# A decoder trunk on one core: loads in another order, first sums of the second group earlier, low halves between norm steps

## The chip, the cores and the metric

The kernel runs on one core of a Trainium2 chip. A core has TensorE (PE) for matrix products, VectorE (DVE), ScalarE (ACT), GpSimd (POOL) and SyncE (SP), which here only issues transfers. Each engine works through its own instructions in order; semaphores order them against each other. The metric is device time in microseconds (us), the median of several executions.

## The reference

The function is a trunk of two layers over 256 tokens of width 1024. Each layer is an FFN, a mixer, and a second FFN, each between two RMS norms and added to x:

```python
hdn = swiglu(rms_norm(x, norm_pre[l, 0]), ffn1_w_gate[l], ffn1_w_up[l], ffn1_w_down[l])
x = x + 0.5 * rms_norm(hdn, norm_post[l, 0])
h = rms_norm(x, norm_pre[l, 1])
...
x = x + rms_norm(mix, norm_post[l, 1])
hdn = swiglu(rms_norm(x, norm_pre[l, 2]), ffn2_w_gate[l], ffn2_w_up[l], ffn2_w_down[l])
x = x + 0.5 * rms_norm(hdn, norm_post[l, 2])

def swiglu(h, w_gate, w_up, w_down):
    return (jax.nn.silu(h @ w_gate) * (h @ w_up)) @ w_down
```

D_FF is 2816. The mixer of layer 0 ("ab") has one input projection to q, k, v (8 heads of 64, causal softmax over the 256 tokens, rotary on a quarter of a head) and to a recurrent group: causal convolution of width 4, a gated linear recurrence, times gelu of a gate branch; one output projection. The mixer of layer 1 ("c") is B * conv3(C * x~) between two projections. All is float32.

## The kernel before, in words

**Precision.** Every float32 operand of a projection is split into a high half (a rounding to fp32r on ScalarE) and a low half (source minus high half on VectorE, L98, `low`). A product is three matmuls: high by high, high by low, low by high (`mm3`, L261 to L263; `proj_a`, L272 to L277, with tokens on the output's partitions, 512 columns wide; `proj_b`, L289 to L291, with features there, 256 wide).

**Weights.** All weights are read once, in chunks of 1 MB, in one list `chunks`, whose order is the order of SP's queue. A chunk lands in one of two rings of raw buffers, 'a' and 'b' (tiles `ra` and `rb`), each of two tiles. `low` frees a raw tile as soon as its low half is made and then calls `pump`, which issues the next chunks (L89) as long as the next one's ring has a free tile. Since the queue keeps the order of the list, a chunk whose own ring has room still goes after the one ahead of it. Five pairs of high and low halves exist (HL). `prep` makes the high half of the next chunk (ACT, L126), and puts its low half on a list `late`; `flush` issues what is on that list. `done(i, n)` gives a pair back and lets `prep` make up to n further ones.

**FFN.** The 2816 hidden features are 11 column blocks of 256. Blocks 0 and 1 are computed in `first(t)`, once for each half t of the tokens; blocks 2 to 10 in a loop over j in `rest`: gate by `proj_b`, tanh on ACT (L449), t1 (L451) on VectorE, up by `proj_b`, h (L460), and then a part of the down product. For the first eight blocks of w_down rows the down product is a scheme of seven products of half-size blocks instead of eight, for which sums of row blocks and of h blocks are needed. `mix(j)` makes the sums of h (L363, L364, L366) and their halves (M and e). `add(i)` makes the sums of the rows: L143 and L144 on VectorE, then two accumulating transfers on POOL's queue (L145, L146), one after the other. `begin(i)` makes their high halves on ACT (L151, L152). `five(b)`, in the loop at j = b + 2, does five of the products, 15 matmuls of 512 columns. The other two (`two`) and the plain down products of blocks 8 to 10 (`plain`) follow as the second group, in the last blocks and in `tail`. In each turn of the loop, VectorE's order ends with `five(j-2)`'s successor `add(d1[j])` for the rows two blocks on.

**Mixers.** In "ab" the scores are made for the first half of tokens, then for the second (`score`), with softmax on ACT (L616), VectorE (L618) and POOL (L619); the gelu of the gate branch (L580 to L585) reads its product from a PSUM bank; v is a `proj_a`, and heads are then transposed and multiplied (`turn_p`). `bank()` hands out PSUM banks from a list `ring` in turn. Outside of these, `stile`, `etile` and `ptile` hand out SBUF tiles in turn. In "c", `first` ends with zz (L771), which the transposition for the convolution reads.

**Norms and boundaries.** `post_add` (L229, L231) adds a stage's normed output to x, `pre_norm` (L239) norms x for the next stage, `trans_x` (L246, L253, L258) transposes it into high and low halves `xh`, `xl`, and `close` (L408) adds the two groups of products. The gains `gpre` and `gpost` are read by a transfer that gives each of the 128 partitions a copy of the row (`load_gain`, L211).

## Time and profile before

| | |
|---|---|
| median of 3 runs | 1074.96 us (1074.94 to 1082.31) |
| profiled execution | 1072.48 us |
| its span | 1070.7 us |
| mean granted clock of TensorE | 0.961 |
| TensorE busy | 960.1 us (90%) |
| VectorE busy | 737.7 us (69%) |
| ScalarE busy | 503.1 us (47%) |
| GpSimd busy | 103.9 us (10%) |

The span is cut by the stages: FFN of layer 0 to about 257 us, mixer "ab" to 396, FFN to 567, FFN of layer 1 to 767, mixer "c" to 885, FFN to the end; the first 28 us of a stage hold the norms and `first`. A row of the timeline is start, duration, engine, line, operation, tiles by name without numbers, and in brackets the idle time of the engine just before, with what ended it. Matmuls overlap, so their rows give durations longer than their distances. The granted clock falls to half in stretches after TensorE stood.

### The profile page before, as it was taken

How to read it: one execution, taken by the hardware profiler on the slowest of the kernel's cores; microseconds unless marked ns; L12 is line 12 of the kernel's file. 1: busy time of each engine (PE TensorE's matmuls, PEld its weight loads, DVE VectorE, ACT ScalarE, POOL GpSimd, SP SyncE). 2: the span in 40 equal slices, each digit the busy share in tenths (PEclk: the TensorE clock that was granted, in tenths of full speed). 3: DMA queues.
4: the chain of work that ended last, by engine and by line, in shares of the span. 5: the costliest groups of instructions: out<-in, count | busy, mean ns of one | idle time of the engine just before them, and what ended most of it. 6: DMA issues, size and time to landing. Idle time of an engine off the chain costs nothing.

```text
span 1070.7 us, 14796 instructions
## 1 busy us (share of the span) xinstructions
PE 960.1 (90%) x6084; PEld 855.4 (80%) x6084; DVE 737.7 (69%) x833; ACT 503.1 (47%) x594; POOL 103.9 (10%) x129
## 2 busy tenths in 40 slices
PE   6868788799988997999998979999989999799997
PEld 4767677787776887988986978898769988798895
DVE  5456654677767857787768667777767586687675
ACT  5432343355594644454464543455543354444541
POOL 3101000000025001010000001100000010010000
PEclk9997889899998999999999989999999999899999
DMA  9565556488523366778775677786855455778851
GB/s 325 143 187 147 157 161 199 119 299 281 198 98 102 119 216 187 234 203 251 246 256 182 180 224 194 234 257 227 275 175 209 164 177 154 223 216 244 242 198 62
DMA packets 132052, 213.24 MB, mean 199 GB/s; under 512 B 4630, under 2 KB 90646, under 8 KB 131984
## 3 DMA queue, kind: packets, MB, share of 16 engines
q1 hardware_dynamic: 122368, 195.05, 52.8%
q0 software_dynamic: 9616, 17.24, 10.1%
q8 instruction: 48, 0.79, 0.3%
q14 instruction: 20, 0.16, 0.0%
HBM read 194.44 MB, written 1.05 MB: 183 GB/s over the span
## 4 chain that ended last, share of the span: by engine, by line
PE 41%; DMA 23%; DVE 19%; issue 8%; ACT 6%; SPq 1%; POOL 1%; DVEq 0%; POOLq 0%; ACTq 0%
DMA rb<-in_ffn_w_down_dram 17%; DVE lo L98 11%; PE b L289 6%; PE b L291 6%; PE b L290 6%; PE b L262 4%; PE b L263 4%; PE b L261 4%; PE b L277 3%; PE b L272 3%; PE b L273 3%; ACT hi L126 2%; DMA rb<-rb 2%; DMA gpre<-in_norm_pre_dram 2%; DVE P L143 2%
## 5 line engine op out<-in xcount | busy, mean ns | idle before, releaser
L291 PE MATMUL b<-xh,lo 128*128 128x256 f32 x1344 | 376.2, 280 | 5.8 <-DVE lo L98 5.8
L289 PE MATMUL b<-xh,hi 128*128 128x256 f32 x1344 | 377.7, 281 | 4.0 <-ACT hi L126 1.6
L290 PE MATMUL b<-xl,hi 128*128 128x256 f32 x1344 | 375.6, 279 | 0.0
L98 DVE TENSOR_TENSOR lo<-ra,hi 128x2048 fp32r<-128x2048 f32 (+1 forms) x115 | 250.7, 2184 | 52.7 <-ACT hi L126 51.3
L289 PEld LDWEIGHTS b<-xh,hi 128*128 128x128 f32 x1344 | 253.2, 188 | 7.2 <-DVE s L771 2.0
L291 PEld LDWEIGHTS b<-xh,lo 128*128 128x128 f32 x1344 | 253.2, 188 | 6.7 <-DVE lo L98 6.7
L290 PEld LDWEIGHTS b<-xl,hi 128*128 128x128 f32 x1344 | 252.4, 188 | 1.7
L126 ACT CAST hi<-ra 128x2048 fp32r<-128x2048 f32 x107 | 203.6, 1903 | 10.9 <-DMA ra<-in_ffn_w_down_dram 3.4
L262 PE MATMUL b<-lo,M 128*128 128x512 f32 x272 | 115.7, 425 | 56.8 <-DVE lo L98 56.8
L98 DVE TENSOR_TENSOR lo<-rb,hi 128x2048 fp32r<-128x2048 f32 (+1 forms) x74 | 155.8, 2112 | 10.8 <-ACT hi L126 10.8
L365 ACT CAST M<-H 128x640 fp32r<-128x640 f32 x32 | 23.3, 728 | 222.8 <-DVE H L364 222.8
L261 PE MATMUL b<-hi,M 128*128 128x512 f32 x272 | 111.8, 411 | 5.6 <-ACT hi L151 5.6
L262 PEld LDWEIGHTS b<-lo,M 128*128 128x128 f32 x272 | 54.3, 200 | 75.5 <-DVE lo L98 64.0
L263 PE MATMUL b<-hi,M 128*128 128x512 f32 x272 | 112.5, 413 | 0.0
L272 PE MATMUL b<-hi,xh 128*128 128x512 f32 x208 | 86.4, 415 | 8.3 <-DVE e L585 8.3
L143 DVE TENSOR_TENSOR P<-rb 128x512 f32<-128x512 f32 x32 | 22.1, 690 | 104.0 <-DMA rb<-in_ffn_w_down_dram 104.0
L273 PE MATMUL b<-lo,xh 128*128 128x512 f32 x208 | 85.9, 413 | 0.5 <-DVE lo L98 0.5
L151 ACT CAST hi<-rb 128x2048 fp32r<-128x2048 f32 x32 | 61.0, 1905 | 24.4 <-DMA rb<-rb 18.1
L126 ACT CAST hi<-rb 128x2048 fp32r<-128x2048 f32 x35 | 66.7, 1905 | 6.9 <-DMA rb<-in_ffn_w_down_dram 6.1
L261 PEld LDWEIGHTS b<-hi,M 128*128 128x128 f32 x272 | 54.1, 199 | 18.1 <-ACT hi L151 6.2
L145 POOL DMA_DIRECT2D rb<-rb x32 | 27.9, 871 | 403.4 <-DVE s L451 267.2
L263 PEld LDWEIGHTS b<-hi,M 128*128 128x128 f32 x272 | 54.6, 201 | 12.2
(185 smaller groups left out, 1065.4 us busy)
## 6 DMA issues: line engine op xcount, KB each, us to landing
rb<-in_ffn_w_down_dram SPq DMA_DIRECT2D x46, 1024.0 KB, 7.7
ra<-in_ffn_w_gate_dram SPq DMA_DIRECT2D x39, 1024.0 KB, 5.6
ra<-in_ffn_w_up_dram SPq DMA_DIRECT2D x39, 1024.0 KB, 5.7
rb<-rb POOLq DMA_DIRECT2D x64, 256.0 KB, 3.7
ra<-in_ffn_w_down_dram SPq DMA_DIRECT2D x14, 1024.0 KB, 5.0
rb<-in_c_w_in_dram SPq DMA_DIRECT2D x6, 1024.0 KB, 6.3
ra<-in_c_w_in_dram SPq DMA_DIRECT2D x6, 1024.0 KB, 6.7
rb<-in_ab_w_in_dram SPq DMA_DIRECT2D x5, 1024.0 KB, 6.5
```

Source lines behind the costliest of these rows:

```text
L98: eng.tensor_tensor(dst_lo, src, src_hi.bitcast(FT), op=OP.subtract)
L126: act.copy(hi[i], raw[i])
L143: dve.tensor_tensor(t3[i], r[:, 3], r[:, 1], op=OP.add)
L151: act.copy(hi[i], raw[i])
L261: pe.matmul(o, sh, mh, start=start, stop=False)
L262: pe.matmul(o, sh, ml, start=False, stop=False)
L263: pe.matmul(o, sl, mh, start=False, stop=stop)
L272: pe.matmul(o, xh[:, n * 4 + k, ts], hi[i][:, k], start=n * 4 + k == 0, stop=False)
L273: pe.matmul(o, xh[:, n * 4 + k, ts], lo[i][:, k], start=False, stop=False)
L289: pe.matmul(o[:, c], hi[i][:, k, cs], xh[:, k], start=k == 0, stop=False)
L290: pe.matmul(o[:, c], hi[i][:, k, cs], xl[:, k], start=False, stop=False)
L291: pe.matmul(o[:, c], lo[i][:, k, cs], xh[:, k], start=False, stop=k == KT - 1)
```

## The change

It has seven parts.

1. In the list of chunks, the rows of w_down for a block stand between its gate and its up, and those of the second block (d1[1]) stand ahead of the gate of j = 3. They were last of the three.
2. `first(1)` prepares one more gate, without its low half at once, and does `add(d1[1])`; `mix(1)` and a flush move to the front part of the turn j = 2; `add(d1[1])` was in that turn.
3. `flush` can issue a given number of low halves, and such calls stand between the steps of the norms at the boundaries; several `done` calls no longer issue their low halves at once.
4. The gains of the next stage are loaded after `first(1)` (`gpre`, `gpost`), no more at the boundary.
5. At the start, the gain of the first norm is one row, copied to all partitions by two matmuls with a row of ones into PSUM, with eight transpositions of the identity ahead of them; it was a transfer to 128 partitions.
6. The mixers' small parameters are loaded on SP's queue in the turns j = 3 and 4 (`hooks`), not on POOL's at the start; their arithmetic is spread over four turns, up to seven small VectorE steps each.
7. In mixer "ab", `ring` is [7, 4, 6, 5] for v and the heads; the second softmax's scaling is eight VectorE steps and no POOL steps; a low half that POOL made (`flush(pool)`) is made by VectorE later. In mixer "c", zz goes ahead of two low halves.

The diff, cut to what the prediction speaks of:

```diff
-    def flush(eng=dve):
-        while late:
+    def flush(eng=dve, n=99):
+        while late and n:
             low(*late.pop(0), eng)
+            n -= 1
...
         for j in range(2, NB):
-            gu[j] = (cols8(wg, j * 256, "a"), cols8(wu, j * 256, "a"))
-            if j - 2 < NS:
+            if j == 3:
+                d1[1] = rows7(wd, 1)
+            g = cols8(wg, j * 256, "a")
+            if j - 2 < NS and j != 3:
                 d1[j - 2] = rows7(wd, j - 2)
+            gu[j] = (g, cols8(wu, j * 256, "a"))
...
             if t == 1:
                 done(g01[0], n=1)
-                done(g01[1], n=0)
                 turn(0)
+                done(g01[1], n=1, now=False)
+                add(d1[1])
...
                 begin(d1[0])
+                flush()
...
                 mix(0)
                 flush()
-                prep()
...
-                dve.scalar_tensor_tensor(t1, th, 1.0, g, op0=OP.add, op1=OP.mult)
-                flush()
                 if j == 2:
-                    add(d1[1])
-                done(gu[j][0], n=1)
+                    flush()
+                    done(gu[j][0], now=False, n=1)
+                    dve.scalar_tensor_tensor(t1, th, 1.0, g, op0=OP.add, op1=OP.mult)
+                    mix(1)
+                    flush()
+                else:
+                    dve.scalar_tensor_tensor(t1, th, 1.0, g, op0=OP.add, op1=OP.mult)
+                    flush()
+                    done(gu[j][0], n=1)
...
                     flush()
-                    if j == 2:
-                        mix(1)
...
-                done(dn[b])
+                done(dn[b], now=b < NB - 1)
...
-            done(d2[4])
+            done(d2[4], now=False)
+            flush(n=1)
...
+            def scale(n):
+                for _ in range(n):
+                    e, r = scales.pop(0)
+                    dve.tensor_scalar(e, e, r, None, op0=OP.mult)
...
-            def after():
-                done(cg[1], hold=True)
-                flush(pool)
-                lru(0)
-
-            gelu(p, after)
+            gelu(p, lambda: scale(4))
+            scale(4)
+            lru(0)
...
+            ring[:] = [7, 4, 6, 5]
             vs = [etile(512) for _ in range(2)]
...
-                done(gc01[0])
-                done(gc01[1])
+                done(gc01[0], now=False)
+                done(gc01[1], now=False)
...
-    load_gain(gpre, npre[0, 0])
+    act.dma_start(row, npre[0, 0:1])
...
+    gain = [bank("y00"), bank("y01")]
+    for n in range(8):
+        pe.transpose(gain[n // 4][:, 0:128], ident, ident)
+    for h in range(2):
+        pe.matmul(gain[h], ones, row[:, h * 512:h * 512 + 512], start=True, stop=True)
...
+        if n < len(subs) - 1:
+            load_gain(gpre, npre[(n + 1) // 3, (n + 1) % 3])
+        if n:
+            load_gain(gpost, npost[n // 3, n % 3])
         s["rest"]()
...
-            if not last:
-                load_gain(gpre, npre[(n + 1) // 3, (n + 1) % 3])
...
-        done(left)
+        flush(n=1)
+        done(left, now=False)
...
-            load_gain(gpost, npost[(n + 1) // 3, (n + 1) % 3])
             xn = pre_norm(1)
+            flush()
```

What that makes of the queues is seen in three places. SP's queue in the first FFN's blocks, before (`ra` and `rb` are the two raw rings):

```order
L89 DMA ra_453<-in_ffn1_w_gate_dram 128x8x256
L89 DMA ra_539<-in_ffn1_w_up_dram 128x8x256
L89 DMA rb_541<-in_ffn1_w_down_dram 128x2x1024
L89 DMA ra_622<-in_ffn1_w_gate_dram 128x8x256
L89 DMA ra_714<-in_ffn1_w_up_dram 128x8x256
L89 DMA rb_716<-in_ffn1_w_down_dram 128x2x1024
```

And SP's queue of the changed kernel in the same blocks, with the small parameters among the weights:

```order
L89 DMA ra_459<-in_ffn1_w_gate_dram 128x8x256
L89 DMA rb_461<-in_ffn1_w_down_dram 128x2x1024
L89 DMA ra_549<-in_ffn1_w_up_dram 128x8x256
L89 DMA ra_621<-in_ffn1_w_gate_dram 128x8x256
L89 DMA rb_623<-in_ffn1_w_down_dram 128x2x1024
L895 DMA e_688<-in_lru_conv_w_dram 4x512
L895 DMA e_688<-in_lru_conv_b_dram 1x512
L895 DMA e_688<-in_lru_gate_a_b_dram 1x512
L895 DMA e_688<-in_lru_gate_x_b_dram 1x512
L895 DMA e_688<-in_lru_lambda_dram 1x512
L895 DMA e_688<-in_c_conv_w_dram 6x512
L89 DMA ra_712<-in_ffn1_w_up_dram 128x8x256
```

The number behind a tile counts up with the program's instructions, so nearly equal numbers mean two transfers that one step lets go: before, up and rows (539, 541), now gate and rows (459, 461).

VectorE's order in the first turns of the third FFN stage, before (L98 are the low halves, `rb_4831` the rows of the second block):

```order
L98 TENSOR_TENSOR lo_4870<-rb_4647,hi_4869 128x2048
L98 TENSOR_TENSOR P_4872<-P_4791,P_4871 128x512
L98 TENSOR_TENSOR M_4907<-H_4833,M_4907 128x640
L98 TENSOR_TENSOR e_4908<-H_4833,e_4908 128x256
L98 TENSOR_TENSOR lo_4919<-ra_4709,hi_4918 128x2048
L451 SCALAR_TENSOR_TENSOR s_4950<-s_4948,b5_4875 128x512
L143 TENSOR_TENSOR P_4952<-rb_4831 128x512
L144 TENSOR_TENSOR rb_4831<-rb_4831 128x512
L98 TENSOR_TENSOR lo_4958<-ra_4829,hi_4957 128x2048
L460 SCALAR_TENSOR_TENSOR H_5014<-s_4950,b7_4965 128x2x256
```

VectorE's order there in the changed kernel, where `rb_4723` holds the rows of the second block:

```order
L418 SCALAR_TENSOR_TENSOR s_4841<-s_4840,b6_4815 128x512
L98 TENSOR_TENSOR lo_4845<-ra_4708,hi_4844 128x2048
L143 TENSOR_TENSOR P_4862<-rb_4723 128x512
L144 TENSOR_TENSOR rb_4723<-rb_4723 128x512
L428 SCALAR_TENSOR_TENSOR s_4892<-s_4841,b4_4867 128x512
L98 TENSOR_TENSOR lo_4860<-ra_4738,hi_4859 128x2048
L98 TENSOR_TENSOR lo_4895<-rb_4647,hi_4894 128x2048
L98 TENSOR_TENSOR P_4897<-P_4810,P_4896 128x512
```

The sums of the second block's rows (L143, L144) stood in the turn j = 2, behind t1; they now stand in `first(1)`, between t1 and hs of the token half (L418, L428).

SP's queue in the second FFN's blocks, before:

```order
L89 DMA ra_3441<-in_ffn2_w_gate_dram 128x8x256
L89 DMA ra_3513<-in_ffn2_w_up_dram 128x8x256
L89 DMA rb_3515<-in_ffn2_w_down_dram 128x2x1024
L89 DMA ra_3596<-in_ffn2_w_gate_dram 128x8x256
L89 DMA ra_3668<-in_ffn2_w_up_dram 128x8x256
L89 DMA rb_3670<-in_ffn2_w_down_dram 128x2x1024
```

And SP's queue there in the changed kernel:

```order
L89 DMA ra_3460<-in_ffn2_w_gate_dram 128x8x256
L89 DMA rb_3527<-in_ffn2_w_down_dram 128x2x1024
L89 DMA ra_3534<-in_ffn2_w_up_dram 128x8x256
L89 DMA ra_3615<-in_ffn2_w_gate_dram 128x8x256
L89 DMA rb_3682<-in_ffn2_w_down_dram 128x2x1024
L89 DMA ra_3689<-in_ffn2_w_up_dram 128x8x256
```

Here up and rows were let go by one step (3513, 3515); now rows go at a step of their own (3527), a few instructions ahead of up (3534).

More of the change, by code (lines that the diff above doesn't have):

```diff
@@ L231, in post_add, with pre_norm @@
             dve.scalar_tensor_tensor(xres[t][:, cs[h]], yg[h], r, xres[t][:, cs[h]], op0=OP.mult, op1=OP.add)
-    def pre_norm(t, then=None):
+    def pre_norm(t, then=None, gain=None):
+        gain = gain or [gpre[:, 0:512], gpre[:, 512:1024]]
         xn = [stile() for _ in range(2)]
@@ L238, in pre_norm @@
         for h in range(2):
[L239 to L240 removed]
+            dve.scalar_tensor_tensor(xn[h], xres[t][:, h * 512:h * 512 + 512], r, gain[h], op0=OP.mult, op1=OP.mult)
         return xn
@@ L545, in rest @@
         def rest():
-            ring[:] = [4, 5, 6, 7]
             xc = []
@@ L610, in score, with softmax @@
                         soft.append((e, mx, per, nk))
-            def softmax():
+            scales = []
+            def softmax(eng=None):
                 while soft:
@@ L618, in softmax @@
                     dve.reciprocal(mx[:, 2], mx[:, 1])
-                    pool.tensor_tensor(e, e, mx[:, 2, :, None].to_broadcast([128, per, nk]), op=OP.mult)
+                    if eng is None:
+                        scales.extend((e[:, n], mx[:, 2, n:n + 1]) for n in range(per))
+                    else:
+                        eng.tensor_tensor(e, e, mx[:, 2, :, None].to_broadcast([128, per, nk]), op=OP.mult)
+            def scale(n):
+                for _ in range(n):
+                    e, r = scales.pop(0)
+                    dve.tensor_scalar(e, e, r, None, op0=OP.mult)
             gates, decay = [], [stile((128, 2, SEQ)) for _ in range(2)]
@@ L649, in between @@
                 gate(1)
-                softmax()
+                softmax(pool)
                 gate2(1)
@@ L724, in rest @@
                         split(m[2][0], m[2][1], ge[0])
+                        done(cg[1], hold=True)
                         scan(1)
@@ L816, in rest @@
         def rest():
-            ring[:] = [4, 5, 6, 7]
             gate(0)
@@ L835, in trunk @@
     act.activation(mhalf, mhalf, AF.Copy)
+    row = gpre[0:1]
+    ones = st.tile([1, 128], FT, name="ones")
+    pool.memset(ones, 1.0)
     for h in range(2):
         sp.dma_start(xres[0][:, h * 512:h * 512 + 512], x[0, 0:128, h * 512:h * 512 + 512])
-    load_gain(gpre, npre[0, 0])
+    act.dma_start(row, npre[0, 0:1])
     dma()
@@ L843, in trunk @@
     make_identity(nc, ident)
-    xn = pre_norm(0)
+    gain = [bank("y00"), bank("y01")]
[3 more added lines that the diff above has]
+        pe.matmul(gain[h], ones, row[:, h * 512:h * 512 + 512], start=True, stop=True)
+    xn = pre_norm(0, gain=gain)
     need(0)
@@ L849, in trunk @@
     pieced(4)
-    xn = pre_norm(1, lambda: (need(2), pieced(4)))
+    xn = pre_norm(1, lambda: (need(2), pieced(4)), gain)
     need(3)
@@ L893, in params, with step @@
         pool.tensor_tensor(a[:, 3], a[:, 2], a[:, 1], op=OP.pow)
-    def params2():
-        a = spw
-        dve.tensor_scalar(a[:, 4], a[:, 3], 2.0, None, op0=OP.add)
-        dve.reciprocal(a[:, 4], a[:, 4])
-        dve.tensor_tensor(a[:, 4], a[:, 3], a[:, 4], op=OP.mult)
-        dve.tensor_tensor(a[:, 5], a[:, 4], a[:, 4], op=OP.mult)
-        dve.memset(a[:, 6], 1.0 / 17)
-        for n in (15, 13, 11, 9, 7, 5, 3, 1):
-            dve.tensor_tensor(a[:, 6], a[:, 6], a[:, 5], op=OP.mult)
-            dve.tensor_scalar(a[:, 6], a[:, 6], 1.0 / n, None, op0=OP.add)
-        dve.tensor_tensor(a[:, 6], a[:, 6], a[:, 4], op=OP.mult)
-        dve.tensor_scalar(a[:, 7], a[:, 0], 0.0, 2.0, op0=OP.max, op1=OP.mult)
-        dve.scalar_tensor_tensor(sp2, a[:, 6], 4.0, a[:, 7], op0=OP.mult, op1=OP.add)
-        dve.tensor_scalar(sp4, sp2, -2.0, None, op0=OP.mult)
-    hooks += [lambda: None, params, params2]
+    a = spw
+    steps = [lambda: dve.tensor_scalar(a[:, 4], a[:, 3], 2.0, None, op0=OP.add),
+             lambda: dve.reciprocal(a[:, 4], a[:, 4]),
+             lambda: dve.tensor_tensor(a[:, 4], a[:, 3], a[:, 4], op=OP.mult),
+             lambda: dve.tensor_tensor(a[:, 5], a[:, 4], a[:, 4], op=OP.mult),
+             lambda: dve.memset(a[:, 6], 1.0 / 17)]
+    for odd_n in (15, 13, 11, 9, 7, 5, 3, 1):
+        steps += [lambda: dve.tensor_tensor(a[:, 6], a[:, 6], a[:, 5], op=OP.mult),
+                  lambda n=odd_n: dve.tensor_scalar(a[:, 6], a[:, 6], 1.0 / n, None, op0=OP.add)]
+    steps += [lambda: dve.tensor_tensor(a[:, 6], a[:, 6], a[:, 4], op=OP.mult),
+              lambda: dve.tensor_scalar(a[:, 7], a[:, 0], 0.0, 2.0, op0=OP.max, op1=OP.mult),
+              lambda: dve.scalar_tensor_tensor(sp2, a[:, 6], 4.0, a[:, 7], op0=OP.mult, op1=OP.add),
+              lambda: dve.tensor_scalar(sp4, sp2, -2.0, None, op0=OP.mult)]
+    def step():
+        for _ in range(min(7, len(steps))):
+            steps.pop(0)()
+    hooks += [lambda: None, loads1, loads2, params, step, step, step, step]
     then = None
```

34 lines of the change are left out of this document (18 added, 16 removed).

## The prediction

> **What bounds the kernel now.** I began with the page's busy table, then cut the span into stages with the table of stretches, then asked which waits TensorE ends on, and last read single places on the timeline.
>
> ```profile
> PE 960.1 (90%) x6084; PEld 855.4 (80%) x6084; DVE 737.7 (69%) x833; ACT 503.1 (47%) x594; POOL 103.9 (10%) x129
> ```
>
> TensorE is the bound: 960.1 of 1070.7 us busy. What can be won is the 110.6 us in which it stands, and the time in which it runs at half clock. The table of stretches shows where both lie (stretch, its length, busy us of PE, PEld, DVE, ACT, POOL, then granted clock, DMA share, GB/s):
>
> ```profile
> 38.00:200.00 162.00, 120.59 (x784) 110.03 (x784) 91.69 (x128) 56.40 (x55) 13.15 (x15) 0.86 0.55 161
> 200.00:257.00 57.00, 54.72 (x336) 48.03 (x335) 40.66 (x34) 32.08 (x31) 1.50 (x2) 1.00 0.68 245
> 257.00:285.00 28.00, 24.03 (x106) 18.82 (x105) 20.92 (x32) 12.19 (x17) 1.57 (x4) 1.00 0.63 206
> 285.00:339.00 54.00, 45.40 (x312) 40.96 (x312) 42.76 (x55) 38.92 (x81) 19.65 (x11) 0.94 0.44 151
> 396.00:432.00 36.00, 29.52 (x210) 27.57 (x209) 26.42 (x33) 14.37 (x16) 3.45 (x4) 0.91 0.66 195
> 432.00:567.00 135.00, 131.52 (x897) 120.11 (x896) 99.38 (x98) 70.47 (x66) 10.15 (x12) 1.00 0.74 234
> 567.00:595.00 28.00, 25.40 (x107) 19.85 (x106) 20.74 (x24) 9.72 (x18) 3.18 (x4) 0.94 0.61 186
> 595.00:634.00 39.00, 32.61 (x228) 30.28 (x227) 27.75 (x36) 17.70 (x20) 3.44 (x4) 0.91 0.67 195
> 634.00:767.00 133.00, 130.40 (x893) 119.55 (x893) 98.72 (x96) 69.64 (x65) 10.05 (x12) 1.00 0.75 236
> 767.00:797.00 30.00, 25.73 (x108) 19.70 (x106) 19.56 (x21) 12.79 (x19) 1.56 (x6) 0.94 0.59 194
> 885.00:930.00 45.00, 37.98 (x252) 34.38 (x251) 30.42 (x37) 19.81 (x23) 4.29 (x5) 0.92 0.61 174
> 930.00:1063.50 133.50, 130.15 (x887) 119.00 (x885) 94.42 (x93) 61.82 (x58) 9.50 (x11) 1.00 0.67 205
> ```
>
> The first FFN's column blocks (38 to 200) are the outlier: 41 us idle, clock 0.86. The three later FFN stages (396 to 567, 595 to 767, 885 to 1063.5) lose 6 to 7 us at their first blocks and about 3 after. The table of waits of TensorE (line, what it waited for, us in total, times, longest) names the ends:
>
> ```profile
> PE b L262 <- DVE lo L98: 58.6, 21, 7.2
> PE b L246 <- DVE s L239: 14.4, 4, 9.1
> PE b L272 <- DVE e L585: 8.3, 1, 8.3
> PE b L277 <- DVE xl L258: 5.3, 3, 1.8
> ```
>
> More than half of the idle time is L262 inside `five`, waiting for the low half of its rows of w_down. Why VectorE is late with it, the timeline of VectorE, SyncE's queue and TensorE shows in one block of the first stage (the row at 137.59 is from the chain of waits, the next block's rows):
>
> ```profile
> 123.49 0.69 DVE L143 TENSOR_TENSOR P<-rb 128x512 f32<-128x512 f32 x1 [7.95 <-DMA rb<-in_ffn_w_down_dram]
> 125.42 2.28 DVE L98 TENSOR_TENSOR lo<-rb,hi 128x2048 fp32r<-128x2048 f32 x1
> ...
> 115.56 0.37 SPq L89 DMA_DIRECT2D ra<-in_ffn_w_up_dram  x1
> 116.03 0.52 SPq L89 DMA_DIRECT2D rb<-in_ffn_w_down_dram  x1
> ...
> 137.59 7.51 DMA rb<-in_ffn_w_down_dram
> ...
> 127.76 0.79 PE L262 MATMUL b<-lo,M 128*128 128x512 f32 x1 [6.25 <-DVE lo L98]
> ```
>
> VectorE is in order. It stands 7.95 us at L143, which adds up rows for a later block, and behind it stands the low half (125.42) which TensorE needs now. The rows were issued at 116.03 only, behind `up` in the same queue, and `up` waited for a buffer that VectorE frees with its low halves. A loop thus closes over VectorE, SP and a transfer of 7.5 us, and one turn of it takes 137.59 − 116.03 = 21.6 us.
>
> **What the change does, part by part.** First the rate of TensorE without gaps, from a later block:
>
> ```profile
> 479.25 0.28 PE L289 MATMUL b<-xh,hi 128*128 128x256 f32 x1
> 490.56 0.39 PE L261 MATMUL b<-hi,M 128*128 128x512 f32 x1
> ...
> 494.71 0.40 PE L263 MATMUL b<-hi,M 128*128 128x512 f32 x1
> 494.94 0.28 PE L289 MATMUL b<-xh,hi 128*128 128x256 f32 x1
> ```
>
> The 96 products of gate and up take 490.56 − 479.25 = 11.31 us, 0.118 each; the last of the 15 products of `five` takes 494.94 − 494.71 = 0.23, so 15 take 3.5, and a column block needs 14.8 us. *First stage.* Seven blocks lie in 38 to 200: 7 × 14.8 = 104, so 58 of the 162 us are waiting or half clock. The change puts the rows between gate and up in SP's queue, and has a further gate prepared in `first`, so that VectorE's early low half frees a buffer for gate and rows together, its late one for up. That is the cadence which the later stages have today for up and rows:
>
> ```profile
> 487.31 0.69 DVE L143 TENSOR_TENSOR P<-rb 128x512 f32<-128x512 f32 x1 [2.08 <-DMA rb<-in_ffn_w_down_dram]
> 489.24 2.28 DVE L98 TENSOR_TENSOR lo<-rb,hi 128x2048 fp32r<-128x2048 f32 x1
> 494.83 0.73 SPq L89 DMA_DIRECT2D rb<-in_ffn_w_down_dram  x1
> 503.74 0.69 DVE L143 TENSOR_TENSOR P<-rb 128x512 f32<-128x512 f32 x1 [2.83 <-DMA rb<-in_ffn_w_down_dram]
> ```
>
> There VectorE still waits 2 to 3 us at L143; the distance of these two L143 is 16.4 us, and 1.6 above 14.8 is the worst residue I allow for a block. I take 0.9 in each of six blocks, 5.4, since gate and rows are asked for half a block before this: −58 + 5 = −53.
>
> *Start.* The half megabyte of gain that every partition read gives way to one row and two matmuls. The first L246 waits 9.1 us in the table of waits; the first weights stood behind the gain's transfer. 0.5 MB at the 245 GB/s of the busiest stretch above is 2.1 us; between nothing and that I take −1, because the first weights bind next: −54 with the stage. The parameter loads, now on SP between weights, are a few kilobytes each; their cover is the weights' lead of half a block; uncovered they cost one more wait of the kind above at L143, 2 to 3 us, once.
>
> *Later stages.* The first rows of the second block were waited for in `five(1)`: 36.00 − 29.52 = 6.5 us in 396 to 432, 6.4 in 595 to 634, 7.0 in 885 to 930. The clock of 0.91 there is 3.2 us of lost full-rate time, about half of it in the wait itself, so 1.7 more each. The change loads and adds these rows up in `first`, a whole stage ahead. Then the blocks: idle 3.5, 2.6 and 3.35. The rows now follow their own ring: they can go when lo<-rb is done (489.24 + 2.28 = 491.52) and not at 494.83, 3.3 us earlier, against 2.08 and 2.83 us of waiting at L143. What is late next is nothing by this row, with only 0.5 us to spare in the second. Sums: −11.6, −10.7 and −12.0. What was moved ahead has a follower: the two accumulates by POOL must land before the ACT copy that the next block's low half needs, 14.8 + 0.7 − 1.9 = 13.6 us after L144 (a block, one VectorE step of 0.7 as L143's, the copy L151). Their rows:
>
> ```profile
> rb<-rb POOLq DMA_DIRECT2D x64, 256.0 KB, 3.7
> 445.88 8.51 DMA rb<-rb
> L151 ACT CAST hi<-rb 128x2048 fp32r<-128x2048 f32 x32 | 61.0, 1905 | 24.4 <-DMA rb<-rb 18.1
> L145 POOL DMA_DIRECT2D rb<-rb x32 | 27.9, 871 | 403.4 <-DVE s L451 267.2
> 440.57 0.86 POOL L145 DMA_DIRECT2D rb<-rb  x1 [12.89 <-DVE s L451]
> 440.49 2.28 DVE L98 TENSOR_TENSOR lo<-rb,hi 128x2048 fp32r<-128x2048 f32 x1
> ```
>
> Two at the median of 3.7 with their issues of 0.9 are 9.2 us: 4.4 to spare. One at 8.51 beside one at 3.7 is 14.0, 0.4 too long; both slow is a rival below. The Trainium skill ("SBUF — State Buffer", section "SBUF: two separate sides") warns that a DMA issued by GpSimd starves of descriptors while VectorE holds their shared port: 620 ns alone became 3100 ns. By that price, 2.5 us more on each of two accumulates, an estimate from that page, a block would lack 0.6 us, some 11 us over 18 blocks. The issue at 440.57 lies inside the low half that began at 440.49 and took 0.86, as the mean of 32 does (871 ns); so here the trace speaks against it, and the sum leaves it out.
>
> *Boundaries.* Gains are loaded after `first`, and low halves stand between the steps of the norm. Idle is 4.0 (257 to 285), 2.6 (567 to 595) and 4.3 (767 to 797), with 0.06 of 28 and 30 us of clock, 1.7 each. The waits L246 and L277 end on VectorE's order, which the change turns, yet part of the norm's own chain stays. Between none and all of 4.0, 4.3 and 6.0, I take −2.6, −3.3 and −5.1: about 1 us stays at each. The tail of the second group (200 to 257) has 2.3 idle, the wait for its first sums, of which I take −2. The Trainium skill ("TensorE: Matmul & The Clock Gate", "Part 1: The HAM clock gate") has the half clock follow a whole idle window of about 3.4 us, so that shorter gaps cost their length alone. In 567 to 595 the clock was 0.94 though no wait there is above 1.8 us; by the page the two 1.7 would not hang on these waits and the gain would be 3.4 smaller.
>
> *Attention.* The wait of 8.31 us for L585 is one for a PSUM bank:
>
> ```profile
> 324.67 0.69 DVE L585 SCALAR_TENSOR_TENSOR e<-e,b 128x512 f32<-128x512 f32 x1 [0.35 <-ACT e L584]
> 325.50 0.77 PE L272 MATMUL b<-hi,xh 128*128 128x512 f32 x1 [8.31 <-DVE e L585]
> ```
>
> The product of v wrote into the bank that still held the gelu's input. It now takes banks 7 and 4, free by then. The wait and 1.5 us of half clock (0.06 of 54, half in the wait) go. A low half leaves POOL for VectorE, later, and POOL's scaling of the softmax becomes eight VectorE steps of half L585's size, 8 × 0.4 = 3.2 us; VectorE is busy 42.76 of the 54 us, so they fit, but the low half may be waited for before the output product: between 0 and its 2.28 us, I take 1.2. −8.3 − 1.5 + 1.2 = −8.6.
>
> **Sum.** −54 − 2 − 2.6 − 8.6 − 11.6 − 3.3 − 10.7 − 5.1 − 12.0 = −110. The profiled execution took 1072.48 us (span 1070.7 and 1.8 around it), so 962.5; the median of the runs is 2.5 above it, so 965. The last 7.2 us (final norm and store) don't change. Bounds of this case: without the residues (5.4 in the first stage, 3.7 at the boundaries and the tail, 1.2 in attention, 1.1 at the start) 11.4 less, 953.6. With the first stage's residue of 0.9 also in 18 blocks of the later stages (six in each behind `five(1)`), 16, and half of the 11 at the boundaries lost, 987.
>
> **The rivals.** *The later stages don't gain.* If the accumulates, or SP's order, take over from rows, `five(1)` and the pitch of today stay in three stages: 34 us of the gain go, 965 + 34 = 999. For it: VectorE's 0.5 us to spare above, and DMA shares of 0.75 that rise as the blocks get shorter. Against: the rows are freed 3.3 us earlier by their own ring. Chance 0.11. *The accumulates bind.* If both take 8.51, a block lacks 2 × (0.9 + 8.5) − 13.6 = 5.2 us, over 18 blocks 94: 1059. For it, the one row at 8.51; against, a median of 3.7 over 64. Chance 0.03. *The phase slips the other way* and the kernel is slower: if in the later stages the gate ahead of the rows in SP's queue waits for the late low half, rows start half a block later and the loop of the first stage opens there, 21.6 us a turn and not 14.8: 6.8 × 18 = 122, so 1087; it decides from 110 / 18 = 6.1 us a block on. Against it: the queue's order has the rows of these stages issued right after the low half of their own ring. Chance 0.03. *The change doesn't reach the first stage*: its loop stays with another transfer at its end, 53 lost, 1018; against, `add` of the next rows then stands behind a transfer asked for half a block earlier. Chance 0.04.
>
> **How the numbers follow.** The forecast has 0.76: 965 us, in 953 to 987. Two of the rivals together, some 1065 to 1080, have 0.03. To leave out no more than 2 in 10, the range goes on past the first rival: 953 to 1001 holds about 0.72 of the forecast's 0.76 and 0.10 of the rival's 0.11. One per cent, about 11 us, is what a measurement of this kernel can tell from no change: faster takes the forecast and the rivals at 999, 1018 and 1059, 0.76 + 0.11 + 0.04 + 0.03 = 0.94; same is the pair, 0.03; slower is the slipped phase, 0.03.
>
> **What would show it.** Right: blocks of the first stage 15 to 16 us apart; no wait above 2 us at the low half in `five(1)`; later blocks 14.8 to 15.2 apart; v's first product without a wait; TensorE idle under 35 us in all, mean clock 0.98 or more, and busy time down to about 935 since half-clock products are gone. Wrong: an L143 that still waits 3 us or more in the later stages, or ACT's copy of the rows waiting for the second accumulate in most blocks.

## The result, and the profile after

The changed kernel takes 957.32 us (median; 955.97 to 958.94) where the kernel before takes 1074.95: a ratio of 0.889, 95% interval 0.885 to 0.894. The profiled execution is 958.94 us with a span of 957.2, 113.5 less than before. The page's busy table of the changed kernel (its lines are numbered anew; L262 to L264 are `mm3`, L290 to L292 `proj_b`):

```profile
PE 937.6 (98%) x6096; PEld 841.2 (88%) x6096; DVE 734.2 (77%) x842; ACT 503.1 (53%) x594; POOL 87.0 (9%) x113
```

TensorE stands 19.6 us of the span where it stood 110.6. It is also busy 22 us less, with twelve instructions more: the mean granted clock is now 0.997 and was 0.961, so that fewer products run at half clock. The table of stretches, cut at the products where the stages begin (stretch, length, busy us of PE, PEld, DVE, ACT, POOL, clock, DMA share, GB/s):

```profile
47.60:173.70 126.10, 120.90 (x894) 113.58 (x893) 96.28 (x127) 57.65 (x53) 13.03 (x16) 1.00 0.77 230
173.70:203.20 29.50, 27.23 (x111) 21.35 (x111) 23.44 (x20) 19.78 (x18) 1.49 (x2) 0.94 0.71 249
203.20:230.60 27.40, 27.33 (x126) 21.89 (x125) 21.21 (x32) 14.05 (x20) 1.51 (x4) 1.00 0.58 192
330.20:461.50 131.30, 130.74 (x989) 124.71 (x989) 103.44 (x111) 63.97 (x63) 12.05 (x14) 1.00 0.82 245
486.70:515.70 29.00, 27.77 (x130) 22.28 (x129) 23.11 (x26) 14.86 (x22) 3.16 (x4) 1.00 0.64 200
515.70:645.90 130.20, 130.20 (x990) 124.77 (x989) 103.46 (x111) 65.17 (x63) 12.11 (x14) 1.00 0.81 247
671.00:698.60 27.60, 27.60 (x130) 22.26 (x128) 17.25 (x20) 15.85 (x22) 1.56 (x6) 1.00 0.59 191
791.30:921.50 130.20, 130.20 (x989) 124.64 (x988) 103.35 (x111) 64.01 (x63) 12.11 (x14) 1.00 0.81 243
```

In the blocks of two FFN stages TensorE has no gap at all. Of the 19.6 us, 7.5 are the end (norm and store, after the last product), 5.2 lie in the first stage's blocks and 2.3 in its second group (173.7 to 203.2, the one stretch of these below full clock). Measured between the same products in both traces, against the terms of the prediction's sum:

| from first product of ... to ... | before, us | after, us | difference | predicted |
|---|---|---|---|---|
| span's start, to first projection | 10.87 | 8.96 | −1.9 | −1 |
| first projection, to second group of the first FFN | 214.93 | 164.80 | −50.1 | −53 |
| second group, to boundary | 27.96 | 29.42 | +1.5 | −2 |
| boundary into mixer ab | 31.53 | 27.39 | −4.1 | −2.6 |
| mixer ab, attention and output | 81.74 | 72.30 | −9.4 | −8.6 |
| second FFN's blocks | 143.08 | 131.26 | −11.8 | −11.6 |
| boundary into layer 1 | 32.52 | 28.95 | −3.6 | −3.3 |
| third FFN's blocks | 142.49 | 130.20 | −12.3 | −10.7 |
| boundary into mixer c | 35.53 | 27.54 | −8.0 | −5.1 |
| fourth FFN, `first` and blocks | 171.53 | 157.68 | −13.8 | −12.0 |

The sum is −113.5, where −110 was predicted; stretches that are not in the table changed by 0.1 us at most. The table of waits of TensorE has shrunk to this (its first three lines; L263 is `mm3`, here in `five` and the second group, L867 the transpositions of the identity at the start, L273 the first product of `proj_a`):

```profile
PE b L263 <- DVE lo L98: 7.8, 7, 1.9
PE b L867 <- POOL ident masks.py:199: 1.6, 1, 1.6
PE b L273 <- DVE s L418: 1.2, 1, 1.2
```

### The profile page after: what moved, and what is told of

Same layout as the page of the kernel before. It is cut to its first block, busy times and chain, and to the rows that moved or that the text cites. A ratio compares the mean times of both kernels' runs of the same rounds, so it can differ in the third digit from the quotient of the medians.

```text
span 957.2 us, 14823 instructions
## 1 busy us (share of the span) xinstructions
PE 937.6 (98%) x6096; PEld 841.2 (88%) x6096; DVE 734.2 (77%) x842; ACT 503.1 (53%) x594; POOL 87.0 (9%) x113
## 4 chain that ended last, share of the span: by engine, by line
PE 73%; DVE 11%; DMA 8%; issue 4%; ACT 2%; POOL 1%; SPq 1%; POOLq 0%; DVEq 0%; ACTq 0%
PE b L290 13%; PE b L291 13%; PE b L292 13%; PE b L263 7%; PE b L264 7%; PE b L262 7%; DVE lo L98 6%; DMA rb<-in_ffn_w_down_dram 5%; PE b L278 4%; PE b L274 4%; PE b L273 4%; DMA rb<-rb 2%; PE b L247 1%; ACT hi L126 1%; POOL ss L222 1%
## 5 line engine op out<-in xcount | busy, mean ns | idle before, releaser
L290 PE MATMUL b<-xh,hi 128*128 128x256 f32 x1344 | 376.5, 280 | 0.0
L292 PE MATMUL b<-xh,lo 128*128 128x256 f32 x1344 | 375.6, 279 | 0.3 <-DVE lo L98 0.2
L98 DVE TENSOR_TENSOR lo<-ra,hi 128x2048 fp32r<-128x2048 f32 (+1 forms) x115 | 250.9, 2186 | 40.7 <-ACT hi L126 39.6
L290 PEld LDWEIGHTS b<-xh,hi 128*128 128x128 f32 x1344 | 252.5, 188 | 2.1 <-issue 0.3
L292 PEld LDWEIGHTS b<-xh,lo 128*128 128x128 f32 x1344 | 251.9, 187 | 1.0 <-DVE lo L98 1.0
L98 DVE TENSOR_TENSOR lo<-rb,hi 128x2048 fp32r<-128x2048 f32 (+1 forms) x75 | 158.1, 2115 | 10.2 <-ACT hi L126 10.2
L263 PE MATMUL b<-lo,M 128*128 128x512 f32 x272 | 108.4, 399 | 5.5 <-DVE lo L98 5.5
L262 PE MATMUL b<-hi,M 128*128 128x512 f32 x272 | 107.7, 396 | 0.0
L264 PE MATMUL b<-hi,M 128*128 128x512 f32 x272 | 107.4, 395 | 0.0
L369 ACT CAST M<-H 128x640 fp32r<-128x640 f32 x32 | 23.3, 729 | 148.9 <-DVE H L368 143.2
L273 PE MATMUL b<-hi,xh 128*128 128x512 f32 x208 | 83.6, 402 | 1.2 <-DVE s L418 1.2
L274 PE MATMUL b<-lo,xh 128*128 128x512 f32 x208 | 83.8, 403 | 0.5 <-DVE lo L98 0.5
L151 ACT CAST hi<-rb 128x2048 fp32r<-128x2048 f32 x32 | 61.1, 1909 | 25.1 <-DMA rb<-rb 20.8
L263 PEld LDWEIGHTS b<-lo,M 128*128 128x128 f32 x272 | 51.0, 188 | 18.8 <-DVE lo L98 7.9
L264 PEld LDWEIGHTS b<-hi,M 128*128 128x128 f32 x272 | 51.1, 188 | 11.9
L262 PEld LDWEIGHTS b<-hi,M 128*128 128x128 f32 x272 | 51.1, 188 | 11.1 <-issue 0.2
L278 PE MATMUL b<-hi,xl 128*128 128x512 f32 x208 | 57.6, 398 | 0.1
```

The lines of the kernel that those rows point to most:

```text
L98: eng.tensor_tensor(dst_lo, src, src_hi.bitcast(FT), op=OP.subtract)
L151: act.copy(hi[i], raw[i])
L262: pe.matmul(o, sh, mh, start=start, stop=False)
L263: pe.matmul(o, sh, ml, start=False, stop=False)
L264: pe.matmul(o, sl, mh, start=False, stop=stop)
L273: pe.matmul(o, xh[:, n * 4 + k, ts], hi[i][:, k], start=n * 4 + k == 0, stop=False)
```

## The experiments

All times are medians; each kernel was timed together with the kernel before, which took 1074.45, 1076.62 and 1077.01 us in the three groups of runs. A difference of 2 or 3 us between kernels of different groups is therefore no more than noise by the times alone, and six of the twelve ratios have 95% intervals that overlap with that of the changed kernel, 0.885 to 0.894 (no further gate, rows first, both boundary kernels, rings shifted, one more chunk early). There the distances between the same products in the traces carry the reading. Pitch is the distance of the first products of two successive `five`, read from the timeline; gap-free it is 14.8 us. It shows how much one block costs:

| kernel | first stage | second FFN |
|---|---|---|
| before | 17.0 24.6 23.4 22.8 22.7 21.7 22.7 | 16.9 21.2 14.8 16.1 15.4 15.7 16.4 |
| after | 14.8 14.8 15.7 17.2 17.3 16.9 14.8 | 14.8 14.8 15.2 14.8 15.5 14.8 14.8 |
| rows last | 14.8 22.7 21.0 21.1 22.6 21.1 21.4 | 14.8 14.8 15.5 15.4 16.1 15.1 16.5 |
| rows not early | 15.2 17.6 15.5 18.3 15.7 16.8 14.8 | 14.8 15.1 14.8 15.9 14.8 14.8 14.8 |
| old list whole | 18.8 21.2 23.3 20.5 22.9 20.2 22.1 | 14.8 17.4 16.1 15.8 16.2 15.5 16.6 |
| rows first in first FFN | 14.8 14.8 15.3 14.9 14.8 14.8 14.8 | 14.8 14.8 14.8 14.8 14.8 14.8 14.8 |
| a third sum | 19.7 14.8 19.1 18.0 21.1 17.8 20.2 | 15.3 20.7 19.9 16.7 20.4 14.8 16.3 |

**Does the list's order make the gain in the blocks?** Rows behind up again, from the fourth block's turn on:

```diff
-            if j - 2 < NS and j != 3:
-                d1[j - 2] = rows7(wd, j - 2)
+            if j == 2:
+                d1[0] = rows7(wd, 0)
             gu[j] = (g, cols8(wu, j * 256, "a"))
+            if 3 < j < NS + 2:
+                d1[j - 2] = rows7(wd, j - 2)
```

> The changed kernel with one edit: from the fourth block on, the rows of w_down stand behind gate and up in the list again (the rows of the second block keep their early place). Theory (the order of the list drives the gain in the column blocks): in the first stage the loop over VectorE, SP and the rows' transfer closes again, about 20 us a block instead of 14.8 to 17.2 on five or six blocks, 20 to 30 us; in the three later stages about 1 us a block comes back, 3 to 6 us each; in all 985 to 1005 us. Rival (the further gate prepared in first, and the second block's rows, are what helps): 957 to 965 us.

1006.08 us, 48.8 more than the changed kernel, ratio to before 0.937 (0.934 to 0.939). VectorE's L143 in the changed kernel, then in this one (groups by line: count, busy, mean ns, idle before and what ended it), then one block of this kernel's first stage on the timeline:

```profile
L143 DVE TENSOR_TENSOR P<-rb 128x512 f32<-128x512 f32 x32 | 22.0, 686 | 15.3 <-DMA rb<-in_ffn_w_down_dram 15.3
```

```profile
L143 DVE TENSOR_TENSOR P<-rb 128x512 f32<-128x512 f32 x32 | 22.1, 690 | 85.1 <-DMA rb<-in_ffn_w_down_dram 85.1
85.18 0.69 DVE L143 TENSOR_TENSOR P<-rb 128x512 f32<-128x512 f32 x1 [7.67 <-DMA rb<-in_ffn_w_down_dram]
77.54 0.39 SPq L89 DMA_DIRECT2D ra<-in_ffn_w_up_dram  x1
78.05 0.52 SPq L89 DMA_DIRECT2D rb<-in_ffn_w_down_dram  x1
```

The loop is back with up ahead of rows and 7.67 us of waiting, at 21 to 23 us a block, with the further gate and the early second block still in place. So in the first stage the order carries most of the gain: from the first `five` to the second group this kernel gives back 33.4 of the 43.5 us won there, and the rival falls. In the later stages' blocks it gives back less than half, 3.5 to 4.8 of 11.8 to 12.9 us each.

**Does the wait in `five(1)` go because the second block's rows come early?** The opposite edit: the order stays, but the second block's rows stand behind their gate, and are added up in their turn:

```diff
-            if j == 3:
-                d1[1] = rows7(wd, 1)
...
-                add(d1[1])
...
                     dve.scalar_tensor_tensor(t1, th, 1.0, g, op0=OP.add, op1=OP.mult)
+                    add(d1[1])
                     mix(1)
```

> The changed kernel, but the second block's rows stand behind the gate of their turn in the list, and are added up in that turn, no more in first. Theory: TensorE waits about 6.5 us at the low half in five(1) of each of the three later stages, and loses 1.7 us more at half clock, 25 us; in the first stage some 5 to 9 us; in all 982 to 992 us. Rival (with rows ahead of up the transfer is early enough by itself): 957 to 963 us.

965.11 us, 7.8 more (its profiled execution, the fastest, shows 3.2 of that), where 982 to 992 was expected. `five(1)` hardly waits: the second pitch is 14.8 to 15.9 in the later stages. It doesn't wait in the kernel with late rows either. Both orders back, the old list whole:

> The changed kernel with the old list whole (gate, up, rows in every turn, the second block's rows too, and these added up in their turn, not in first). Taken singly, late rows cost 49 us and the second block's rows 8 us. Theory (each of the two orders by itself is enough against the wait in five(1); only without both does the second block's transfer stand behind two others): that wait of about 6.5 us with its half clock is back in three later stages, 25 us beyond late rows alone, 1006 + 25 + 2 to 8 in the first stage = 1033 to 1040 us. Rival (the wait in five(1) was one of VectorE's order in first and of mix(1), which stay changed): 1010 to 1016 us.

1020.0 us, between the two expectations. `five(1)` in the second FFN, before and in this kernel, on the timeline of TensorE:

```profile
428.07 0.79 PE L262 MATMUL b<-lo,M 128*128 128x512 f32 x1 [4.51 <-DVE lo L98]
```

```profile
397.22 0.50 PE L263 MATMUL b<-lo,M 128*128 128x512 f32 x1 [2.31 <-DVE lo L98]
```

So more than one edit shares this wait. The early second block is enough, rows ahead of up is enough, and without both, 2.3 of the 4.5 us come back (14 us in the whole kernel against rows last, 3 to 4 per stage). The old list whole gives back 37.6 of the 43.5 us in the first stage's blocks, and 7.6 to 7.8 of the 11.8 to 12.9 us in those of each later stage. The rest there, some 4 to 5 us a stage, and the 16.9 us of the first pitch, of which these three kernels show nothing in the later stages, went with what these kernels still had changed. `mix(1)` and the flush in the front part of that turn are a guess that wasn't tried apart.

**Why 17 us in three blocks of the first stage?** In the changed kernel the rows wait there for the gate ahead of them in SP's queue (timeline of VectorE and of SP's queue):

```profile
77.95 2.28 DVE L98 TENSOR_TENSOR lo<-ra,hi 128x2048 fp32r<-128x2048 f32 x1
90.82 0.69 DVE L143 TENSOR_TENSOR P<-rb 128x512 f32<-128x512 f32 x1 [3.99 <-DMA rb<-in_ffn_w_down_dram]
95.55 2.29 DVE L98 TENSOR_TENSOR lo<-ra,hi 128x2048 fp32r<-128x2048 f32 x1
80.27 0.39 SPq L89 DMA_DIRECT2D ra<-in_ffn_w_gate_dram  x1
80.76 0.63 SPq L89 DMA_DIRECT2D rb<-in_ffn_w_down_dram  x1
98.35 1.13 SPq L89 DMA_DIRECT2D rb<-in_ffn_w_down_dram  x1
```

From L143 (90.82) to the end of lo<-ra (97.84) are 7.0 us, and the rows issued at 80.76 were there at 90.8, 10.0 later: 17 us a turn. The list with rows ahead of the gate in that stage alone:

```diff
-            if j == 3:
-                d1[1] = rows7(wd, 1)
+            lead = j == 3 or j > 3 and min(d1.values()) < 32
+            if lead and j - 2 < NS:
+                d1[j - 2] = rows7(wd, j - 2)
             g = cols8(wg, j * 256, "a")
-            if j - 2 < NS and j != 3:
+            if j - 2 < NS and not lead:
                 d1[j - 2] = rows7(wd, j - 2)
```

> The changed kernel, but in the first FFN alone the rows stand ahead of the gate of their turn from the fifth block on, so that they wait for their own ring only and not for the raw tile that the gate needs. Theory (three blocks of 17.2 us come from the rows' issue behind the low half of up: VectorE's 7.0 us from L143 to that low half and 10 us of landing make 17.2): the rows go about 2.8 us earlier and alone, the blocks take 14.8 to 15, 6 to 8 us less, 949 to 952 us. Rival (the transfers themselves limit, 230 GB/s in that stretch, with the small parameter loads among them): 955 to 959 us.

950.78 us, ratio 0.885 (0.883 to 0.888), 6.5 less than the changed kernel, as the theory had it. The same places in it, with all 32 of L143 in the first row:

```profile
L143 DVE TENSOR_TENSOR P<-rb 128x512 f32<-128x512 f32 x32 | 21.9, 684 | 0.0
72.98 2.28 DVE L98 TENSOR_TENSOR lo<-rb,hi 128x2048 fp32r<-128x2048 f32 x1
75.34 0.39 SPq L89 DMA_DIRECT2D rb<-in_ffn_w_down_dram  x1
78.09 0.37 SPq L89 DMA_DIRECT2D ra<-in_ffn_w_gate_dram  x1
84.57 0.69 DVE L143 TENSOR_TENSOR P<-rb 128x512 f32<-128x512 f32 x1
```

Rows go 0.1 us after their own ring's low half ends (75.26), and L143 waits no more anywhere.

**The further gate in `first`.** Without it (`done(g01[1], n=0)`, and `prep()` at the end of the second token half's transposition, as before):

> The changed kernel, but in first no further gate is prepared (as before: one after the second token half's transposition, in the second turn). Theory (order of the list alone sets where rows are issued): the first stage keeps 15 to 17.5 us a block, 956 to 964 us. Rival (the preparation one step ahead sets which of VectorE's two low halves in a turn lets gate and rows go, as the prediction had it): the first stage's blocks go to about 21 us, and the later stages lose their 14.8 too, 980 to 1010 us.

967.53 us, 3.5 above the upper end of what the theory gave, and far from the rival. The pitches stay as in the changed kernel (14.8 to 17.5 in the first stage). What is lost are two waits ahead of the first `five`, 3.3 and 1.8 us, with half clock behind the first, in its table of waits (L290 and L292 are `proj_b`):

```profile
PE b L290 <- ACT hi L126: 3.3, 1, 3.3
PE b L292 <- DVE lo L98: 2.0, 2, 1.8
```

So the further gate is worth 8.0 us at the start (first `five` at 55.57 and not 47.59) and sets no cadence; the prediction credited it with a share of that.

**How near is the chain of accumulates?** A third transfer of the same size, of zeros, between the two:

```diff
         pool.dma_start(r[:, 3], r[:, 1], accum_op=OP.add)
+        pool.dma_start(r[:, 3].rearrange("p (a c) -> p a c", a=2), zero[:, None, :].to_broadcast([128, 2, 256]), accum_op=OP.add)
         pool.dma_start(r[:, 2], r[:, 3], accum_op=OP.add)
```

> The changed kernel with a third accumulating transfer of the same size, of zeros, between the two of every block's rows, so that the chain of transfers is half as long again. The median landing is 4.6 us in the changed kernel. Theory (13.6 us from L144 to the copy is the budget, two take 2 x (0.9 + 4.6) = 11.0): three take 16.5, 2.9 too long, which comes back in each of up to 24 blocks, 40 to 70 us, 1000 to 1027 us. Rival (more room than that, since L143 of a block runs ahead of need): 957 to 965 us.

1042.32 us, 85 more, above what even the theory gave. The page's transfers and the copies L152 (L151 before) of this kernel, ahead of them those rows of the changed kernel:

```profile
L151 ACT CAST hi<-rb 128x2048 fp32r<-128x2048 f32 x32 | 61.1, 1909 | 25.1 <-DMA rb<-rb 20.8
rb<-rb POOLq DMA_DIRECT2D x64, 256.0 KB, 4.6
```

```profile
L152 ACT CAST hi<-rb 128x2048 fp32r<-128x2048 f32 x32 | 61.0, 1906 | 150.6 <-DMA rb<-rb 143.8
rb<-rb POOLq DMA_DIRECT2D x64, 256.0 KB, 5.5
rb<-zero POOLq DMA_DIRECT2D x32, 256.0 KB, 4.0
```

A chain is now 2 × 5.5 + 4.0 + 3 × 0.9 = 17.7 us at the medians, 4.1 over the budget of 13.6. Of the 85 us some 57 are waits of TensorE (76.7 us idle and not 19.6), the rest is products at half clock (964.2 us busy and not 937.6); 57 / 4.1 is 14 of the up to 24 blocks. So the chain binds at this length. The budget of 13.6 itself is an estimate that was not measured, and the third transfer also made the other two slower (5.5 and not 4.6 us). In the changed kernel two take 2 × (4.6 + 0.9) = 11.0 of the budget, 2.6 to spare; the prediction had 4.4. The landing time went from 3.7 to 4.6 us as DMA's share rose from 0.74 to 0.82 in the second FFN's blocks.

**Attention.** One line left out (`ring[:] = [7, 4, 6, 5]`):

> The changed kernel with the banks of PSUM in the old order for v and the heads (one line left out). Theory: the first product of v waits for the gelu's last VectorE step again, about 8 us, and 1.5 us more at half clock: 966 to 968 us. Rival (the moved low half and the softmax's scaling freed that bank earlier anyway): 957 to 960 us.

968.08 us, 10.8 more, and 10.4 more between the same products of this mixer. In its waits the old one is back to a tenth (L273 is the first product of v, L593 the gelu's last VectorE step):

```profile
PE b L273 <- DVE e L593: 8.3, 1, 8.3
```

**Boundaries.** Low halves in their old places:

```diff
-                done(dn[b], now=b < NB - 1)
+                done(dn[b])
...
-            done(d2[4], now=False)
-            flush(n=1)
+            done(d2[4])
...
-        flush(n=1)
-        done(left, now=False)
+        done(left)
...
             xn = pre_norm(1)
-            flush()
```

(and the two `done` of mixer c without `now=False`.)

> The changed kernel with the low halves at the boundaries in their old places (each issued as soon as its high half, none between the norm's steps, zz of the mixer c behind two of them). Theory (the waits for xl, for the normed x and for zz came from low halves ahead of them in VectorE's queue): the boundaries into mixer ab, into layer 1, into mixer c and into the last FFN give back most of 4.1 + 3.6 + 8.0 + 0.9 us, 966 to 973 us. Rival (the gains that were loaded at the boundary made these waits): 957 to 960 us.

964.56 us, 7.2 more, 1.4 less than the theory's lower end. And the gains loaded at the boundary, the rest as changed:

> The changed kernel with the gains of both norms loaded at the boundary again, as before. Theory (VectorE's low halves, not these transfers, were late for TensorE): 0 to 3 us more, 957 to 960 us. Rival (the norm's step waits for the gain's transfer of 7 us, and TensorE for it): 3 to 9 us more, 961 to 967 us.

964.98 us, 7.7 more: the theory falls here. The waits of TensorE in the one and the other (L247 is the transposition of the normed x, L241 the norm's last step, L274 a product of `proj_a` with a low half):

```profile
PE b L247 <- DVE s L241: 6.3, 3, 2.3
```

```profile
PE b L274 <- DVE lo L98: 6.5, 4, 2.2
484.22 1.42 DVE L241 SCALAR_TENSOR_TENSOR s<-x,ss,gpre 128x512 f32<-128x512 f32 x2 [3.73 <-DMA gpre<-in_norm_pre_dram]
485.55 2.28 DVE L98 TENSOR_TENSOR lo<-ra,hi 128x2048 fp32r<-128x2048 f32 x1
```

With late gains VectorE stands 3.73 us at the norm, and the low halves behind it come late for the next projection. Between the same products as in the table, the three boundaries take 3.8, 2.4 and 2.2 us more with the low halves in their old places, and 2.0, 2.9 and 2.8 more with late gains. So each part is needed. The two losses are no split of the gain, though: at the first two boundaries they are together more than was won (4.1 and 3.6), and into mixer c 3.0 less than the 8.0. The old waits for `xl` (L277 before, 5.3 us) and for zz (1.6 us) came back in neither kernel, nor did the 0.9 us that `first` of the fourth FFN gained. What ended these was not tried apart, and the two edits together were not run.

**The second group of the first stage.** It waits 0.4 and 1.8 us, in the changed kernel as before (timeline of TensorE, changed kernel):

```profile
177.17 0.50 PE L262 MATMUL b<-hi,e 128*128 128x512 f32 x1 [0.45 <-ACT hi L126]
179.49 0.80 PE L263 MATMUL b<-lo,e 128*128 128x512 f32 x1 [1.83 <-DVE lo L98]
```

First guess: its first rows land in ring a there. (They do so in the third FFN too, at 622.5 us in SP's queue, and not, as the expectation below has it, in the first alone; and there the second group, 645.9 to 671.0, has no gap. That speaks against the guess.) On top of rows first, the rings shifted by one behind the column blocks:

> The kernel with the rows first in the first FFN (950.78 us), and with the rings of the chunks behind the column blocks shifted so that the second group's first rows land in ring b in every FFN stage; in the first FFN alone they landed in ring a, behind up. Theory (the waits of 0.4 and 1.8 us at the start of the second group, and the half clock behind them, which only the first stage has, come from that ring): 3 to 4 us less, 946.5 to 948 us. Rival (they come from VectorE's work ahead, or the shifted rings cost as much in the mixers): 950 to 955 us.

950.96 us, nothing, and both waits stay, 0.45 and 1.83 us. The half clock behind them is gone all the same: the second group takes 28.0 us and not 29.5, and 1.8 us are lost elsewhere, in the next boundary and the second FFN's blocks. The last section comes back to this. Second guess: the first stage prepares one chunk less ahead, so that the high half of the second pair of row blocks is made only when needed. On top of rows first:

```diff
-                    done(gu[j][0], n=1)
+                    done(gu[j][0], n=2 if j == NB - 1 and d1[0] < 32 else 1)
```

> The kernel with the rows first in the first FFN (950.78 us), and with one more chunk prepared in the last turn of the first FFN's loop. Theory (the waits of 0.44 and 1.82 us at the second group, and half clock behind them, which only the first stage has, come from its preparation being one chunk behind the other stages', since one of five pairs stays empty): 3 to 4 us less, 946.5 to 948 us. Rival (the second group's transfers are late themselves): 950 to 952 us.

948.76 us, ratio 0.881 (0.877 to 0.884), the fastest of all, 8.6 less than the changed kernel. Both waits there are gone; one of 0.9 us, further back in the second group, is left. From the second group's first product (167.3) to the boundary (193.6) are 26.4 us at full clock, where rows first alone took 29.5 (the line runs 0.9 us past the boundary):

```profile
167.30:194.50 27.20, 26.28 (x119) 21.00 (x117) 22.70 (x20) 18.08 (x18) 1.49 (x2) 1.00 0.76 276
```

The gain of 2.0 is about half of what was expected: the 3.2 us of the second group include the half clock, 0.9 of waiting stays, and a wait of 0.5 us comes up in the last `five` ahead of it. Does the same lag explain the 17 us blocks? The changed kernel, its list untouched, with one more chunk prepared in `first` of that stage (`done(u01[1], n=1, now=False)`):

> The changed kernel with one more chunk prepared in first of the first FFN alone, the list unchanged. Theory (the first stage's blocks of 17 us and its waits at the second group have one reason, that its preparation runs one chunk behind the other stages'; then the same list gives 14.8 us a block as it does there): 6 to 11 us less, 946 to 951 us. Rival (the small parameter loads and the first stage's transfers make the difference): 955 to 959 us, or more where the further chunk delays VectorE in first.

952.77 us, 4.6 less, between the two expectations: the waits at the second group are gone (25.2 us to the boundary, as in the second and third FFN), but the blocks still take 14.8 to 16.8 us. So the lag makes the waits at the second group, and is a part of the long blocks; for those the order is the better cure.

## Why the prediction was right, point by point

The time, 957.3, lies 7.7 below the forecast of 965 and inside its own narrower range, 953 to 987. Of the 7.7, about 3.6 are in the sum of the terms. The other 4.1 are between executions: the prediction put the median 2.5 above the profiled execution, as before, and it lies 1.6 below. The sum of −110 against −113.5 hides errors of both signs, 6.4 us promised too much and 10.0 too little; that they nearly cancel is luck. The signs it named came, but for two: three blocks of the first stage are 16.9 to 17.3 us apart, and one later block 15.5.

*First stage*, −53 against −50.1: the loop that it named is the one that the rows-last kernel brings back. The step "early low half frees a buffer for gate and rows together, its late one for up" is what the rows at 77.95, 80.27 and 80.76 show. The further gate, which it counted into this cadence, is instead what wins the 6.6 us ahead of the first `five` (45.3 us from the first projection before, 38.6 now, 46.6 without that gate). Mis-sized is the residue, 5.4 against 7.9 in four blocks (15.7, 17.2, 17.3 and 16.9, less 14.8 each): gate and rows asked for together land in 10 us, not in the 8 to 9 that the later stages showed before. With rows ahead of the gate it is 0.6.

*`five(1)`*: size right, reason too narrow. The step "The change loads and adds these rows up in `first`, a whole stage ahead" isn't needed: rows ahead of up do it too, and part of the wait stays away with neither, for a reason that is open.

*Later blocks*: the 3.3 us by which rows go earlier, against 2.08 and 2.83 of waiting, was the right comparison. L143 waits six times in all, and all in the first stage, so the half microsecond to spare was enough.

*Accumulates*: the budget of 13.6 is not contradicted, the cover was overstated, 4.4 where 2.6 are left. The rival that both transfers bind was nearer than its 0.03 said: 2.6 us are left, and with 4.1 us too much in the third-sum kernel the chain binds. It also read one row at 8.51 us, where four of the 64 transfers took over 8 us before; four do now, up to 9.6.

*Second group of the first FFN*, −2 against +1.5: the wrong step. The prediction took the wait for one on the first sums; it is one on a preparation that lags one chunk in that stage, which the change doesn't touch. The +1.5 is no effect of the change either, but half clock that comes and goes between kernels with the same two waits (last section): five of the twelve experiments take 28.0 us there, as before.

*Boundaries*, −11 against −15.7 for the three: the 1 us held back at each was not there, except 1.2 us into layer 1 (L273 waiting for L418). The reason given, low halves in VectorE's order, was a part of it; that the gains come early is another, and the waits for `xl` and zz are not accounted for.

*Clock*: the Trainium skill's page "TensorE: Matmul & The Clock Gate" ("Part 1: The HAM clock gate") has half clock follow a whole idle window of about 3.4 us. By it the gain at the boundaries into layer 1 and mixer c would have been 1.7 us smaller each. They gained 3.6 and 8.0 us, more than their idle time of 2.6 and 4.3, and the clock there went from 0.94 to 1.00. So here half clock did come with waits of 1.8 to 2.3 us, and went with them. The measurement decides.

*Attention*, −8.6 against −9.4: mechanism and size hold; of the 1.2 us kept for the moved low half, one wait of 0.47 us on a low half is seen, in the output product.

The rivals: later stages gain all that was forecast, no phase slipped, and the first stage is reached. The start (−1.9 against −1) and the moved parameter loads were not tried apart.

## What to carry to other kernels

In a queue that issues in order, place a transfer by the buffer it waits for: one with a ring of its own goes ahead of those that wait for a ring still in use, and a turn of the loop "free, issue, land, consume" is then compared with the time of a block. Where VectorE waits in order for such a transfer, everything behind it is late, and what the tensor engine is seen to wait for is that follower. Before shortening a stage, compute what the next chain (here two serial accumulates) has to spare, at the landing times of the busier, faster kernel and not of the slower one.

## What the runs showed of the hardware that was not expected

The half clock doesn't follow from a wait's length alone. At the second group of the first FFN the kernel before has the same two waits as the changed one (timeline of TensorE and stretch to the boundary, before):

```profile
229.20 0.50 PE L261 MATMUL b<-hi,e 128*128 128x512 f32 x1 [0.46 <-ACT hi L126]
231.53 0.50 PE L262 MATMUL b<-lo,e 128*128 128x512 f32 x1 [1.82 <-DVE lo L98]
225.80:253.70 27.90, 25.62 (x110) 20.14 (x109) 20.24 (x18) 18.67 (x18) 1.50 (x2) 1.00 0.78 282
```

There the clock stayed at 1.00; in the changed kernel it is 0.94 over the same products, which is the 1.5 us more in the table. Three waits of 1.3 to 1.9 us in the changed kernel's first stage left it at 1.00 (47.6 to 173.7).

What decides can be read from the traces' record of the granted clock. In each of the 14 traces the clock changes only on a grid of steps of 3.41 us, and the grid lies elsewhere in each execution. Counting by the recorded spans of its products how long TensorE stood in each step at full clock: every step in which it stood for a share of 0.54 or more was followed by a step at half clock, none with a share below 0.44 was, and of the 18 between, 7 were.

| step of the grid, us | share of it in which TensorE stood | clock in the next step |
|---|---|---|
| changed kernel, second group, 175.88 to 179.29 | 0.61 | half |
| rows first, second group, 169.97 to 173.39 | 0.54 | half |
| before, boundary into layer 1, 568.04 to 571.45 | 0.53 | half |
| before, second group, 226.71 to 230.12 and 230.12 to 233.53 | 0.26 and 0.41 | full |
| rings shifted, second group, 167.54 to 170.96 and 170.96 to 174.37 | 0.27 and 0.40 | full |
| changed kernel, the three waits in the first stage's blocks | 0.33, 0.37 and 0.26 at most | full |

So the same two waits of 0.45 and 1.83 us cost half clock where more than about half of one step is idle by them, and no clock where a step's border divides them. A whole idle step is not needed here.

Accumulating transfers issued by POOL land in 4.6 us instead of 3.7, median of all 64, in a kernel whose blocks of the second FFN move 245 instead of 234 GB/s. That the load is the cause was not tried.
